# The low part of a weight block: a subtraction on DVE, or a negated copy on ACT and an adding DMA

## The chip, the cores and the metric

The kernel runs on one core of one Trainium2 chip. The core has a matrix engine (PE), a vector engine (DVE), an activation engine (ACT), a general engine (POOL), an engine that here only issues transfers (SP), and 16 DMA engines that carry the transfers of all queues. Each engine works through its own list of instructions in order; an instruction starts when the semaphores it names have reached their values. The metric is the device time of one execution in microseconds (us), as the median of several runs.

## The reference

Four layers of a transformer over 512 tokens of width 1024, all in float32: two layers with a mixer, a cross attention and a feed-forward network (FFN), then two layers with another mixer and an FFN. Cut to the part that the change is about:

```
def _conv_ffn(h, w_in, conv_w, conv_b, w_out):      # first two layers, D_FF = 2816
    gate, up = split(h @ w_in, 2)
    gate = causal_dwconv(gate, conv_w, conv_b)
    return (gelu(gate) * up) @ w_out

# each of the last two layers (mixer, then FFN of the same width)
    g = sigmoid(gate_logit)                         # three gates of width 1024 from h @ w_in
    merged = g[0] * y_attn + g[1] * y_conv + g[2] * y_pool
    x = x + merged @ w_o
    gt, up = split(rmsnorm(x) @ w_ffn_in, 2)
    x = x + (silu(gt) * up) @ w_ffn_out
```

## The kernel before

**Products in three parts.** Every operand of a large product is cut in two float32r tiles: the high part `hi` (a rounding copy on ACT, L167) and the low part `lo = src - hi` (a subtraction on DVE, L168). A product is then three matmuls, high by high, high by low, low by high (`mm3`, L248). `split` (L166) makes the two parts of any operand.

**Seven products.** The four FFNs and the gates of the two later mixers multiply a 2x2 arrangement of weight blocks with a 2x2 arrangement of activations by a scheme that needs seven block products in place of eight, at the cost of sums of blocks. `plan_seven` (L464) loads four weight blocks of 128x1024 float32 (512 KB each), called g1, g2, u1, u2, makes four sums in place on DVE (`add`, L470: first s1 = u1 + u2, then u1 = g1 - u1 and g1 = s1 - g1, later g2 = g2 - g1) and has seven blocks cut by `cut` (L450): U1 = g1, U2 = g2, U3 = the new g1, U4 = s1, U5 = the new u1, U6 = u2, U7 = the new g2. `seven` (L498) multiplies them one after the other on PE, two column halves of 12 matmuls each, and between them ACT copies partial sums out of PSUM (L512, L521, L528) and DVE adds others to them (L517, L529, L536). In the fifth product the copy L528 takes the sum out of a PSUM tile into which the sixth product then accumulates, so that the sixth product cannot start on a half before that half's L528 is done.

**FFN.** Each pair of hidden blocks is one `seven`, and after each follows `second` (L575), the product of an earlier group's hidden blocks with one or two loaded blocks of `w_out`, called w8 and w9 here. These two are loaded and cut by `unit` (L206), not by `cut`. An FFN has one plain start (four cuts) and ten `seven`; behind the first two of them `second` takes one block, behind the other eight two.

**Buffers.** The raw blocks lie in two rings: "raw" with three buffers (g2, u2, w8, w9 and their like take turns) and "rb" with four (g1, u1, s1). A load is issued on SP (L447 in `block`, L211 in `unit`) once the last reader of its buffer is done. SP's list is in order, so a load that waits holds back those behind it. The cut parts lie in five buffers each ("whi", "wlo"), a sixth one is added in the gates. A cut may start when PE has done with the block five before it.

**Order.** `Feed` keeps four cut units ahead of PE; the scheduler of the language then sets each engine's order once, when the program is built.

Of the kernel before, what the change touches and what calls it, by code (L numbers as in the profile page):

```python
# [9 lines left out]
F32 = mybir.dt.float32  # L10
# [4 lines left out]
AF = mybir.ActivationFunctionType  # L15
ALU = mybir.AluOpType
# [85 lines left out]
class Core:  # L102
# [347 lines left out]
    def cut(self, t):  # L450
        self.turn = (self.turn + 1) % 6
        pool, bufs = (self.extra, 1) if self.extra and self.turn == 0 else (self.wp, 5)
        hi = pool.tile([P, 1024], F32R, tag="whi", name=self.nm("wh"), bufs=bufs)
        lo = pool.tile([P, 1024], F32R, tag="wlo", name=self.nm("wl"), bufs=bufs)
        self.split(hi, lo, t)
        return hi.rearrange("p (k c) -> p k c", k=4), lo.rearrange("p (k c) -> p k c", k=4)

    def prod(self, out, u, c, bh, bl, start=True, stop=True, more=False):
# [1240 lines left out]
```

## Time and profile before

| what | value |
|---|---|
| median of 3 runs | 3035.33 us (3033.89 to 3038.63) |
| profiled execution | 3036.64 us |
| its span, first to last instruction | 3034.9 us |
| PE busy | 2985.4 us, 98% of the span |
| DVE busy | 2265.0 us, 75% |
| ACT busy | 1512.8 us, 50% |
| POOL busy | 66.5 us, 2% |
| DMA traffic | 317.45 MB, 105 GB/s on average |

The span is one execution seen by the profiler; what is missing to the profiled execution's own time (1.7 us) lies before the first and after the last instruction. Busy shares are averages over very different stages. A row of a list by engine gives start, duration, engine, line, operation, output and inputs; in square brackets stands how long the engine was idle before it and whose end released it. The chain of waits is the list of steps, followed back from the last instruction, each of which had to end before the next could start.

### The profile page before, as it was taken

The page shows a single profiled execution, that of the slowest core. Times are in us where ns is not written, and L with a number is a line of the kernel's source. Part 1 is how long each engine was busy: PE and PEld are TensorE (multiplying, and loading weights), DVE is VectorE, ACT ScalarE, POOL GpSimd, SP SyncE. Part 2 cuts the span into 40 slices and gives each one's busy share as a digit, 9 for nine tenths or more (in the row PEclk, how much of TensorE's full clock was granted, in tenths as well). Part 3 has the DMA queues.
Part 4 walks back from the last instruction along what each step waited for, and adds up shares of the span by engine and source line. Part 5 has one row for each costly group of instructions (what it writes and reads, how often), then busy time and mean ns, then how long its engine had stood idle before and what let it go on. Part 6 is the DMA issues. An engine that isn't in the chain of part 4 may idle for free.

```text
span 3034.9 us, 46642 instructions
## 1 busy us (share of the span) xinstructions
PE 2985.4 (98%) x18376; PEld 2613.1 (86%) x18376; DVE 2265.0 (75%) x4188; ACT 1512.8 (50%) x2475; POOL 66.5 (2%) x99
## 2 busy tenths in 40 slices
PE   8999999999999999999999999999999999999999
PEld 6888888999887788899988699899998779889998
DVE  6855768888776676888878588687777768777775
ACT  6634545545544554554454465454445555554442
POOL 1300000000000000000000000000001000000000
PEclk9999999999999999999999999999999999999999
DMA  5122522333332352233334143323334223423332
GB/s 181 36 85 97 178 87 88 103 103 105 100 123 70 105 189 97 74 114 98 105 126 119 31 125 105 129 91 105 103 105 127 87 63 122 132 91 98 104 105 77
DMA packets 232896, 317.45 MB, mean 105 GB/s; under 512 B 10805, under 2 KB 165927, under 8 KB 231781
## 3 DMA queue, kind: packets, MB, share of 16 engines
q1 hardware_dynamic: 224933, 292.20, 30.8%
q0 software_dynamic: 7744, 22.27, 2.3%
q8 instruction: 144, 2.36, 0.3%
q14 instruction: 75, 0.61, 0.1%
HBM read 294.49 MB, written 15.75 MB: 102 GB/s over the span
## 4 chain that ended last, share of the span: by engine, by line
PE 85%; DVE 9%; DMA 3%; ACT 2%; issue 1%; POOL 0%; SPq 0%; DVEq 0%; ACTq 0%
PE mm L248 58%; PE at L248 19%; PE at L203 3%; DVE wl L168 2%; PE at L1210 2%; DVE wr L470 1%; DMA wr<-in_w_ffn_in 1%; DMA wr<-in_ffn_w_in 1%; DMA wr<-in_w_in 1%; ACT wh L167 1%; PE at L696 0%; PE at L853 0%; DMA wr<-in_w_o 0%; DVE big L168 0%; DVE x L546 0%
## 5 line engine op out<-in xcount | busy, mean ns | idle before, releaser
L168 DVE TENSOR_TENSOR wl<-wr,wh 128x1024 fp32r<-128x1024 f32 (+1 forms) x678 | 817.7, 1213 | 311.0 <-ACT wh L167 301.3
L167 ACT CAST wh<-wr 128x1024 fp32r<-128x1024 f32 (+1 forms) x678 | 700.5, 1042 | 523.4 <-PE mm L248 307.4
L248 PE MATMUL mm<-Hh,wh 128*128 128x256 f32 (+1 forms) x2256 | 677.5, 300 | 3.7 <-DVE u L529 2.4
L248 PE MATMUL mm<-Hh,wl 128*128 128x256 f32 (+1 forms) x2256 | 674.5, 299 | 0.0
L248 PE MATMUL mm<-Hl,wh 128*128 128x256 f32 (+1 forms) x2256 | 674.1, 299 | 0.0
L248 PEld LDWEIGHTS mm<-Hh,wh 128*128 128x128 f32 x2256 | 423.8, 188 | 25.5 <-DVE u L529 4.1
L248 PEld LDWEIGHTS mm<-Hl,wh 128*128 128x128 f32 x2256 | 423.8, 188 | 23.6 <-issue 4.9
L248 PEld LDWEIGHTS mm<-Hh,wl 128*128 128x128 f32 x2256 | 425.5, 189 | 19.7 <-issue 2.4
L248 PE MATMUL mm<-wh,Hh 128*128 128x512 f32 x896 | 358.6, 400 | 1.5 <-ACT Hh L167 1.5
L248 PE MATMUL mm<-wh,Hl 128*128 128x512 f32 x896 | 353.8, 396 | 0.8 <-DVE Hl L168 0.8
L248 PE MATMUL mm<-wl,Hh 128*128 128x512 f32 x896 | 353.2, 394 | 0.0
L248 PE MATMUL mm<-big,wh 128*128 128x256 f32 x1920 | 341.8, 280 | 6.3 <-ACT u L528 5.0
L248 PEld LDWEIGHTS mm<-big,wh 128*128 128x128 f32 x1920 | 290.5, 188 | 11.9 <-ACT u L528 6.2
L470 DVE TENSOR_TENSOR wr<-wr,wr 128x1024 f32<-128x1024 f32 x208 | 253.8, 1220 | 53.2 <-DMA wr<-in_w_ffn_in 28.4
L248 PE MATMUL at<-wl,ah 128*128 128x512 f32 x704 | 276.8, 393 | 0.0
L248 PE MATMUL at<-wh,al 128*128 128x512 f32 x704 | 276.0, 392 | 0.0
L248 PE MATMUL at<-wh,ah 128*128 128x512 f32 x704 | 275.2, 391 | 0.0
L248 PE MATMUL mm<-big,wl 128*128 128x256 f32 x960 | 266.6, 278 | 0.4 <-DVE wl L168 0.2
L248 PEld LDWEIGHTS mm<-wh,Hl 128*128 128x128 f32 x896 | 169.0, 189 | 39.7 <-DVE Hl L168 3.1
L248 PEld LDWEIGHTS mm<-wh,Hh 128*128 128x128 f32 x896 | 169.3, 189 | 36.4 <-ACT Hh L167 2.5
L248 PEld LDWEIGHTS mm<-wl,Hh 128*128 128x128 f32 x896 | 169.4, 189 | 35.0
L248 PEld LDWEIGHTS mm<-big,wl 128*128 128x128 f32 x960 | 181.2, 189 | 0.8 <-DVE wl L168 0.8
(407 smaller groups left out, 4317.6 us busy)
## 6 DMA issues: line engine op xcount, KB each, us to landing
wr<-in_ffn_w_in SPq DMA_DIRECT2D x88, 512.0 KB
wr<-in_w_ffn_in SPq DMA_DIRECT2D x88, 512.0 KB
wr<-in_w_in SPq DMA_DIRECT2D x84, 512.0 KB
wr<-in_ffn_w_out SPq DMA_DIRECT2D x44, 512.0 KB
wr<-in_w_ffn_out SPq DMA_DIRECT2D x44, 512.0 KB
wr<-in_ev_w_in SPq DMA_DIRECT2D x32, 512.0 KB
wr<-in_xa_w_kv SPq DMA_DIRECT2D x32, 512.0 KB
wr<-in_od_w_in SPq DMA_DIRECT2D x24, 512.0 KB
```

What stands on the lines that cost most here:

```text
L167: self.nc.scalar.copy(out=hi, in_=src)
L168: self.nc.vector.tensor_tensor(out=lo, in0=src, in1=hi.bitcast(F32), op=ALU.subtract)
L203: return self.nc.tensor.transpose(out=out, in_=in_, identity=self.ident)
L248: return self.nc.tensor.matmul(*args, **kw, skip_group_check=more)
L470: self.nc.vector.tensor_tensor(out=out, in0=a, in1=b, op=op)
L1210: nc.tensor.matmul(out[:, i * P:], lhsT=v[:, i, h * width:(h + 1) * width], rhs=pT[:, OFF[i]:OFF[i] + S - i * P], start=i == 0, stop=i == ...
```

## The change

`cut` no longer calls `split`. ACT makes the high part as before, then writes the negated high part to the low tile (`activation` with `AF.Copy` and scale -1), and then POOL issues a DMA that adds the raw block to that tile in place. `unit`, `split` for activations and all loads stay as they are.

```diff
     def cut(self, t):
         ...
         hi = pool.tile([P, 1024], F32R, tag="whi", name=self.nm("wh"), bufs=bufs)
         lo = pool.tile([P, 1024], F32R, tag="wlo", name=self.nm("wl"), bufs=bufs)
-        self.split(hi, lo, t)
+        nc = self.nc
+        nc.scalar.copy(out=hi, in_=t)
+        nc.scalar.activation(out=lo, in_=hi.bitcast(F32), func=AF.Copy, scale=-1.0)
+        nc.gpsimd.dma_start(out=lo, in_=t, accum_op=ALU.add)
         return hi.rearrange("p (k c) -> p k c", k=4), lo.rearrange("p (k c) -> p k c", k=4)
```

The lines behind the change move down by three (L167 of `cut` becomes L456 and L457, L512 becomes L515, L521 becomes L524, L528 becomes L531). The program now has 380 DMAs of the new kind.

Place 1: ACT in the FFN of the second layer (the other FFNs repeat it), from the cut of U6 to the second L528 of one `seven`. Before (wh2098 is U6's high part, wh2100 U7's, wh2103 and wh2106 those of w8 and w9, wh2112 the next step's U1; wr is the raw block, DMAHW a wait on a load):

```order
L167 CAST wh2098_12975<-wr2072_12788 128x1024 [waits DMAHW6_49,PE_49]
L512 COPY g2092_12927<-mm2091_12926 128x256 [waits PE_49]
L167 CAST wh2100_13005<-wr2070_12784 128x1024 [waits DVE_49,PE_49]
L521 COPY g2089_12911<-mm2088_12910 128x256 [waits PE_49]
L167 CAST wh2103_13034<-wr2102_13033 128x1024 [waits DMAHW7_49,PE_49]
L521 COPY g2092_12927<-mm2091_12926 128x256 [waits PE_49]
L167 CAST wh2106_13068<-wr2105_13067 128x1024 [waits DVE_49,DMAHW2_49,PE_49,Activation_49]
L528 COPY u2090_12912<-mm2088_12910 128x256 [waits PE_49]
L167 CAST wh2112_13105<-wr2108_13097 128x1024 [waits DMAHW0_49,DVE_49,PE_49]
L528 COPY u2093_12928<-mm2091_12926 128x256 [waits PE_49]
```

Now, the same stretch:

```order
L456 CAST wh2098_13079<-wr2072_12887 128x1024 [waits DMAHW6_49,PE_49]
L515 COPY g2092_13030<-mm2091_13029 128x256 [waits PE_49]
L457 ACTIVATE wl2099_13080<-wh2098_13079 128x1024 [waits DMASW0_49,Activation_49]
L456 CAST wh2100_13110<-wr2070_12883 128x1024 [waits DVE_49,PE_49]
L457 ACTIVATE wl2101_13111<-wh2100_13110 128x1024 [waits DMASW1_49,PE_49,Activation_49]
L524 COPY g2089_13014<-mm2088_13013 128x256 [waits PE_49]
L167 CAST wh2103_13140<-wr2102_13139 128x1024 [waits DMAHW7_49,PE_49]
L524 COPY g2092_13030<-mm2091_13029 128x256 [waits PE_49]
L167 CAST wh2106_13174<-wr2105_13173 128x1024 [waits DMAHW2_49,PE_49]
L531 COPY u2090_13015<-mm2088_13013 128x256 [waits PE_49]
L456 CAST wh2112_13211<-wr2108_13203 128x1024 [waits DMAHW0_49,PE_49]
L531 COPY u2093_13031<-mm2091_13029 128x256 [waits PE_49]
```

Behind each cast of a cut stands a negated copy, and the cast of w9 (wh2106) still stands ahead of L531.

Place 2: SP in the same step, the loads of w8 (wr2102), the next g1 and u1 (wr2108, wr2110), w9 (wr2105) and the next g2 and u2 (wr2109, wr2111). Before:

```order
L211 DMA wr2102_13033<-in_ffn_w_out 128x2x512 [waits DMAHW4_49,DVE_49]
L447 DMA wr2108_13097<-in_ffn_w_in 128x4x256
L447 DMA wr2110_13101<-in_ffn_w_in 128x4x256 [waits DMAHW2_49,DVE_49,Activation_49]
L211 DMA wr2105_13067<-in_ffn_w_out 128x2x512 [waits DMAHW6_49,DVE_49]
L447 DMA wr2109_13099<-in_ffn_w_in 128x4x256 [waits DMAHW5_49,DMAHW3_49,DVE_49]
L447 DMA wr2111_13103<-in_ffn_w_in 128x4x256 [waits DMAHW7_49,DVE_49]
```

Now (DMASW is a wait on a DMA that POOL issued):

```order
L211 DMA wr2102_13139<-in_ffn_w_out 128x2x512 [waits DMAHW4_49,DVE_49]
L447 DMA wr2108_13203<-in_ffn_w_in 128x4x256 [waits DMASW5_49]
L447 DMA wr2110_13207<-in_ffn_w_in 128x4x256 [waits DMASW2_49,DMAHW2_49,DVE_49,Activation_49]
L211 DMA wr2105_13173<-in_ffn_w_out 128x2x512 [waits DMAHW6_49,DMASW5_49,Activation_49]
L447 DMA wr2109_13205<-in_ffn_w_in 128x4x256 [waits DMAHW7_49,DMAHW3_49,DVE_49]
L447 DMA wr2111_13209<-in_ffn_w_in 128x4x256 [waits DMAHW5_49,DMASW6_49]
```

The order of the loads is the same; w9's load (wr2105) and u2's (wr2111) wait for an adding DMA where they waited for DVE.

## Rows read from the trace of the kernel before

**Rows 1.** Page, busy us, share of the span, instructions.

```profile
PE 2985.4 (98%) x18376; PEld 2613.1 (86%) x18376; DVE 2265.0 (75%) x4188; ACT 1512.8 (50%) x2475; POOL 66.5 (2%) x99
```

**Rows 2.** Page, the chain that ended last, by line.

```profile
PE mm L248 58%; PE at L248 19%; PE at L203 3%; DVE wl L168 2%; PE at L1210 2%; DVE wr L470 1%; DMA wr<-in_w_ffn_in 1%; DMA wr<-in_ffn_w_in 1%; DMA wr<-in_w_in 1%; ACT wh L167 1%; PE at L696 0%; PE at L853 0%; DMA wr<-in_w_o 0%; DVE big L168 0%; DVE x L546 0%
```

**Rows 3.** Groups of instructions: count, busy us, mean ns, idle before, releasers.

```profile
L168 DVE TENSOR_TENSOR wl<-wr,wh 128x1024 fp32r<-128x1024 f32 (+1 forms) x678 | 817.7, 1213 | 311.0 <-ACT wh L167 301.3
L167 ACT CAST wh<-wr 128x1024 fp32r<-128x1024 f32 (+1 forms) x678 | 700.5, 1042 | 523.4 <-PE mm L248 307.4
L470 DVE TENSOR_TENSOR wr<-wr,wr 128x1024 f32<-128x1024 f32 x208 | 253.8, 1220 | 53.2 <-DMA wr<-in_w_ffn_in 28.4
```

**Rows 4.** Windows: us, busy of PE, PEld, DVE, ACT, POOL; clock, DMA share, GB/s.

```profile
655.60:686.20 30.60, 30.60 (x219) 28.46 (x218) 25.06 (x34) 15.06 (x22) 0.00 (x0) 1.00 0.32 104
655.60:675.00 19.40, 19.40 (x169) 19.25 (x168) 14.00 (x17) 9.50 (x14) 0.00 (x0) 1.00 0.47 154
1743.00:1895.00 152.00, 148.00 (x1119) 139.29 (x1118) 129.74 (x168) 86.96 (x137) 0.00 (x0) 1.00 0.37 111
```

**Rows 5.** ACT in order of time, one step of the first FFN.

```profile
654.84 2.03 ACT L167 CAST wh<-wr 128x1024 fp32r<-128x1024 f32 x2
657.20 0.37 ACT L512 COPY g<-mm 128x256 f32<-128x256 f32 x1 [0.33 <-PE mm L248]
658.45 1.05 ACT L167 CAST wh<-wr 128x1024 fp32r<-128x1024 f32 x1 [0.87 <-PE mm L248]
659.40 0.36 ACT L512 COPY g<-mm 128x256 f32<-128x256 f32 x1
661.17 1.05 ACT L167 CAST wh<-wr 128x1024 fp32r<-128x1024 f32 x1 [1.40 <-PE mm L248]
666.61 1.05 ACT L167 CAST wh<-wr 128x1024 fp32r<-128x1024 f32 x1 [1.40 <-PE mm L248]
668.08 0.37 ACT L528 COPY u<-mm 128x256 f32<-128x256 f32 x1 [0.42 <-PE mm L248]
```

**Rows 6.** DVE in the same step.

```profile
659.53 1.23 DVE L168 TENSOR_TENSOR wl<-wr,wh 128x1024 fp32r<-128x1024 f32 x1 [0.76 <-ACT wh L167]
```

**Rows 7.** SP's DMA issues in the same step.

```profile
660.79 0.37 SPq L211 DMA_DIRECT2D wr<-in_ffn_w_out  x1
```

**Rows 8.** PE in the same step, the start of the sixth product.

```profile
669.24 0.39 PE L248 MATMUL mm<-big,wh 128*128 128x256 f32 x2
```

**Rows 9.** Chain of waits in order of time, an earlier step of that FFN.

```profile
572.03 1.15 DVE wl L168
573.17 0.02 SPq L211
...
573.23 3.65 DMA wr<-in_ffn_w_out
...
577.85 1.03 ACT wh L167
578.88 0.28 ACT u L528
579.16 0.04 issue
579.21 4.37 PE mm L248 x36
```

**Rows 10.** Waits of the SP queue: us in total, times, longest.

```profile
SPq L211 <- DVE wl L168: 801.1, 151, 38.3
SPq L447 <- DVE wl L168: 562.2, 109, 32.3
```

**Rows 11.** DMA issues: count, KB each, median us to landing.

```profile
xd<-x POOLq DMA_DIRECT2D x5, 2048.0 KB, 8.6
mt<-memT POOLq DMA_DIRECT2D x2, 1024.0 KB, 6.0
td<-big POOLq DMA_DIRECT2D x4, 512.0 KB, 3.1
self<-in_c_sel POOLq DMA_DIRECT2D x2, 512.0 KB, 3.8
poolc<-in_c_pool POOLq DMA_DIRECT2D x2, 17.0 KB, 2.2
```

**Rows 12.** DMA queues: packets, MB, share of 16 engines' span.

```profile
q0 software_dynamic: 7744, 22.27, 2.3%
```

**Rows 13.** Waits of PE: us in total, times, longest.

```profile
PE mm L248 <- ACT u L528: 11.3, 11, 2.0
PE mm L248 <- DVE u L529: 2.4, 5, 0.9
```

## The prediction

> **What bounds the kernel now.** I read the page's busy shares first. PE is busy 2985.4 of 3034.9 us, DVE 75%, ACT 50% [rows 1]: 49.5 us are all that PE stands idle. The chain of waits by line says the same: matmuls at L248 take 77% of it, the subtraction that the change removes (DVE wl L168) 2%, the high-part copy 1% [rows 2]. The windows then show one FFN step (a `seven` of 19.4 us, then a `second` of 11.2 us): PE is busy for all of its 30.6 us, DVE for 25.06, ACT for 15.06, and the DMA engines for a third [rows 4]. In that stage DVE has slack already, so taking work from it buys nothing directly. Only in the gates does PE miss time, 4 us of 152 [rows 4].
>
> The waits of the SP queue are the view that matters most: loads waited for "DVE wl L168" 801 and 562 us in total [rows 10]. A raw buffer becomes free when the subtraction has read it, and only then is the next load issued. These waits cost nothing as long as the load still lands in time. The chain in order of time shows where it does not quite: a subtraction ends, SP issues the load of a `w_out` block, the load lands 3.65 us later, ACT casts it (1.03 us), ACT then does the copy L528, and PE starts the sixth product [rows 9]. PE waited for L528 11.3 us in all [rows 13]. This is the path on which the new operation lies.
>
> **What is removed and added.** L470 ran 208 times, four sums to a `seven` [rows 3]: 52 of them with seven cuts each, and four plain starts with four each, are 380 cuts. DVE loses 380 x 1.213 = 461 us [rows 3] and falls to 59% of the span. ACT gains 380 negated copies. None is in the trace; the cast of the same shape took 1.04 us [rows 3], four copies of 128x256 would take 4 x 0.37 = 1.48 us [rows 5], none could be free. I take 1.04, so 395 us, which puts ACT at 63%, and in the gates at (86.96 + 42 x 1.04) / 152 = 86% [rows 4]. Its busy time alone binds nothing, but its order does: in the list each negated copy stands among PSUM copies for which PE waits.
>
> The 380 adding DMAs have no counterpart in the trace. A POOL transfer of 17 KB landed 2.2 us after its issue, 512 KB in 3.1 or 3.8, 1024 KB in 6.0, 2048 KB in 8.6 [rows 11]. So about 2.2 us are fixed, and a pass over 512 KB takes 0.9 to 1.6 us; POOL's queue gives the same upper figure, 22.27 MB in 2.3% of 3034.9 us, 1.64 us for 512 KB [rows 12]. An addition has to read the raw block and also the tile that it adds to, so I count two passes: 1.8 to 3.3 us, and take 2.5, between the two rows of 512 KB doubled. The bounds are one pass (0.9) and three, with the write apart (3 x 1.64 = 4.9).
>
> The Trainium skill bears on this. "Collectives: The Full Stack", section "The bandwidth ceiling: the fold count and why AG ≠ RS ≠ AR", says that the DMA engines' inline addition is not slow by its arithmetic but by its two source reads, which halve the rate; no run here shows it yet. "DMA: Bandwidth & Descriptors", section "Anatomy of one DMA — SWDGE (gpsimd) path", gives about 2.0 us plus bytes at 436 GB/s for a POOL transfer; for 1024 KB that is an estimate of 4.4 us where the trace had 6.0 [rows 11], and 3.2 us for 512 KB beside 3.1. By that figure the pass would be 1.2 us, two of them 2.4, and the sum below would hardly move.
>
> **The FFN step, followed through.** T = 655.6 is the start of a `seven`. Casts of U4 and U5 ran at 654.84, back to back; that of U6 at 658.45, when PE had freed its slot; that of w9 at 666.61; L528 at 668.08; the sixth product began at 669.24 [rows 5, 8]. In the new ACT list a negated copy follows each cast, so: cast U4 to 655.9, its negation to 656.9, cast U5 to 658.0, the PSUM copy to 658.3, negation U5 to 659.4, cast U6 to 660.4, PSUM copy to 660.8, negation U6 to 661.85. Before, U6's subtraction was done at 659.53 + 1.23 = 660.76, and SP issued w9's load at 660.79 [rows 6, 7].
>
> Now the adding DMAs. With 2.2 us fixed and 2.5 us on the engines, one behind the other: U4 lands at 661.6, U5 at 664.1, U6 at 666.6, U7 at 669.1. PE needs the low part of U4 at about 664.1, of U5 at 666.9, U6 at 669.5, U7 at 672.3 (19.4 / 7 = 2.77 us to a product): all in time. What is late is the load behind U6: w9's load goes out at 666.65 instead of 660.79. It lands 3.65 us later [rows 9], plus some 1.2 us since U7's addition has half of the engines then; cast 1.03 and L528 0.28 follow. Sum: 666.65 + 3.65 + 1.2 + 1.03 + 0.36 = 672.9, against 669.24: PE stands still for 3.6 us. Behind the waiting cast of w9 on ACT stand both L528 and the next step's U1; behind w9's load on SP stand the next g2 and u2. The stall recurs, since the chain starts anew at each step when PE frees U6's slot. Break-even is an addition landed 2.3 us after its issue.
>
> Of the 40 FFN steps 32 have a w9: 32 x 3.6 = 115 us. The other eight have no second `w_out` block; I take nothing for them (at most the same, 29 us). DVE's in-place sums must now wait until an addition has read the block; U1's negation ends some 3 us after its cast in the pause before `second`, and I take nothing for it either.
>
> **The gates.** There `seven` follows `seven` with little between. U7's addition lands at T + 13.5; the next load into that buffer lands at T + 18.4; its cast, negation (2.1) and addition (4.7) end at T + 25.2, and the second product of the next `seven` wants it at T + 19.4 + 2.8 = T + 22.2. That is 3 us for each of the 12, 36 us. The engines' own load gives a floor: 0.37 x 152 = 56 us of loads [rows 4] plus 42 x 2.5 = 105 us are 161 us in a stage of 152, 9 us each; the larger figure stands.
>
> **The sum.** 3036.6 us (the profiled execution, 1.3 above the median) + 115 + 36 = 3188; less 1.3 and rounded, 3190 us, 5% slower. With 1.8 us on the engines the same steps give a stall of 2.5 us and 0.8 us in a gate `seven`: 82 + 10, 3128 us. With 3.3 us U6 lands at 669.0, the stall is 6.5 us and a gate `seven` loses 7.4: 207 + 89, 3333 us. So 3125 to 3335 is this case's own range.
>
> **Rivals.** *The DMA engines become the bound.* With 4.9 us for an addition an FFN step needs 0.32 x 30.6 + 7 x 4.9 = 44 us of engines in 30.6 us [rows 4], 13.5 us too many in each of 40 steps, and each gate stage 56 + 206 - 152 = 110 us: 540 + 220, about 3800 us. For it: 380 additions are more than POOL's queue ever carried [rows 12]. Against it: nothing here shows three passes. It decides from about 2.9 us an addition, in the gates from 2.3.
>
> *The addition is cheap and hidden.* At one pass (0.9 us) U6 lands at 664.95, the stall is some 1.2 us: 3075 us. With 2 us more slack than I count (a load that lands sooner, another order on SP) nothing is left and the time stays at 3035. For it speaks that td landed in 3.1 us [rows 11]; against it, that the second operand must be read.
>
> *Faster, by the relief of DVE.* The chain of rows 9 begins with DVE's subtractions. If an addition landed in under 2.3 us, loads would go out earlier than now, the 11.3 and 2.4 us of PE's waits for L528 and L529 [rows 13] would go, and the gates' 2 x 4 us: 3015 us. PE's idle 49.5 us are the limit of any gain.
>
> That the change does not do what it says is excluded by the order of the program.
>
> **Chances and range.** Forecast (3125 to 3335) 0.51; DMA-bound (above 3335) 0.25; cheap and hidden 0.18, of which 0.06 ends within 0.2% of now, about what a measurement of this kernel tells from no change; faster 0.06. So faster 0.06, same 0.06, slower 0.88. The range runs from 3050 to 3650 us: below it lie the faster case and no change, above it the far end of the DMA-bound case.
>
> **What would show it.** In the new profile: PE idle of 100 to 200 us with "ACT u L531" as its foremost releaser; SP's L211 waiting on the adding DMAs; a landing of the new POOL issues between 4 and 7 us; POOL's queue above 20% of the engines; DVE near 60%. Wrong would be the forecast if PE's idle time stood in front of the low parts themselves (a matmul that waits for wl), or if the DMA share were above 90% in the FFN windows.

## The result, and the profile after

The changed kernel takes 3474.29 us (3471.37 to 3478.24, 4 runs) against 3035.69 for the kernel before: 1.1445 times as long, with a 95% interval of 1.1425 to 1.1464. The forecast was 3190 us. The direction held and the time lies inside the range, but the loss is 439 us where 155 were forecast.

On the page of the changed kernel the first line is busy time by engine, then come the queue that carries POOL's transfers and the issues of the adding DMAs with their median landing:

```profile
PE 3120.0 (90%) x18376; PEld 2731.5 (79%) x18376; DVE 1846.7 (53%) x3808; ACT 1860.9 (54%) x2855; POOL 397.7 (11%) x479
...
q0 software_dynamic: 62464, 221.53, 33.0%
...
wl<-wr POOLq DMA_DIRECT2D x380, 512.0 KB, 5.9
```

Beside [rows 1], DVE lost 418 us of work and ACT gained 348. PE does the same 18376 matmuls, yet its busy time rose from 2985.4 to 3120.0 us, and its idle time from 49.5 to 349.6 us (3469.6 of span less 3120.0). These two, 134.6 and 300.1 us, are the whole 434.7 us by which the span grew. PE's waits in the changed kernel (us in total, times, longest) answer to [rows 13]:

```profile
PE mm L248 <- ACT u L531: 191.4, 40, 6.8
PE mm L248 <- DMA wl<-wr: 78.2, 52, 4.7
PE mm L248 <- ACT b L167: 17.7, 4, 5.5
PE mm L248 <- DVE ac L549: 9.9, 5, 3.4
```

The copy named in the forecast leads. Next come waits for the adding DMAs themselves, of which there were none before. The group of matmuls that the FFNs' seven products alone have shows how much of the first row is theirs (count, busy us, mean ns, idle before):

```profile
L248 PE MATMUL mm<-big,wh 128*128 128x256 f32 x1920 | 410.4, 316 | 170.8 <-ACT u L531 165.8
```

So 165.8 of the 191.4 us belong to the FFNs, and 25.6 to the gates. The waits for wl are 22.5 us in the FFNs' seven products, 42.0 us in the gates, and 13.7 us at the FFNs' starts.

The chain of waits in order of time shows one such stall in the third FFN, piece by piece, as [rows 9] does for before:

```profile
2359.95 6.99 DMA wl<-wr
2366.94 0.02 SPq L211
...
2366.99 3.85 DMA wr<-in_w_ffn_out
...
2370.92 0.07 ACT wh L167
...
2371.87 0.37 ACT u L531
...
2372.29 8.36 PE mm L248 x48
```

It reads as forecast: U6's addition lands 6.99 us after its issue, SP issues w9's load, that lands 3.85 us later, ACT casts w9, then copies, then PE starts. PE's own rows put its idle time before that start at 4.14 us:

```profile
2372.29 0.80 PE L248 MATMUL mm<-big,wh 128*128 128x256 f32 x2 [4.14 <-ACT u L531]
```

What PE does then is in the windows (us, busy of PE, PEld, DVE, ACT, POOL with counts, clock, DMA share, GB/s), the first just before the stall, the second just behind it:

```profile
2360.00:2367.90 7.90, 7.90 (x72) 7.90 (x71) 1.65 (x2) 3.61 (x5) 1.69 (x2) 1.00 1.02 191
2372.30:2377.60 5.30, 5.30 (x25) 5.30 (x26) 4.04 (x5) 2.12 (x3) 0.87 (x1) 0.50 0.73 231
```

After 4.14 us at rest the granted clock is at its lower level, 0.50 (1.2 GHz), for 5.3 us: 25 matmuls took 5.3 us, where 72 took 7.9 before. At the earlier pace the 25 would have taken 2.7 us, so the stall costs 2.6 us again as PE busy time. The first copy L531 of two successive steps, in ACT's rows of the first FFN, gives the length of a step:

```profile
679.46 0.37 ACT L531 COPY u<-mm 128x256 f32<-128x256 f32 x1
...
717.04 0.37 ACT L531 COPY u<-mm 128x256 f32<-128x256 f32 x1
```

That is 37.6 us, against 30.6 [rows 4]. The new instructions by group (count, busy us, mean ns, idle before):

```profile
L458 POOL DMA_DIRECT2D wl<-wr x380 | 331.0, 872 | 2208.7 <-ACT wl L457 1446.8
...
L457 ACT ACTIVATE wl<-wh 128x1024 fp32r<-128x1024 f32 x380 | 400.2, 1060 | 6.8 <-issue 2.4
```

The engine time of one addition follows from the queue: 33.0% of 3469.6 us is 1145 us; less the 70 us that the same queue had before [rows 12], divided by 380, it is 2.83 us.

The trace also has the landing of each addition and the time of each DMA packet. In the 40 FFN steps the addition of U3, which finds the queue free, lands 4.55 us after its issue in the median; those of U4 to U7, issued close together, take 4.89, 5.70, 6.23 and 7.09. For the 32 loads of w9, the median time from the issue to the end of the load's last packet is 3.32 us before and 4.70 now.

### The profile page after: what moved, and what is told of

Same layout as the page of the kernel before. It is cut to its first block, busy times and chain, and to the rows that moved or that the text cites. A ratio compares the mean times of both kernels' runs of the same rounds, so it can differ in the third digit from the quotient of the medians.

```text
span 3469.6 us, 48042 instructions
## 1 busy us (share of the span) xinstructions
PE 3120.0 (90%) x18376; PEld 2731.5 (79%) x18376; DVE 1846.7 (53%) x3808; ACT 1860.9 (54%) x2855; POOL 397.7 (11%) x479
## 5 line engine op out<-in xcount | busy, mean ns | idle before, releaser
L168 DVE TENSOR_TENSOR wl<-wr,wh 128x1024 fp32r<-128x1024 f32 (+2 forms) x298 | 358.2, 1204 | 568.7 <-ACT wh L167 558.7
L458 POOL DMA_DIRECT2D wl<-wr x380 | 331.0, 872 | 2208.7 <-ACT wl L457 1446.8
L248 PE MATMUL mm<-big,wh 128*128 128x256 f32 x1920 | 410.4, 316 | 170.8 <-ACT u L531 165.8
L456 ACT CAST wh<-wr 128x1024 fp32r<-128x1024 f32 x380 | 394.2, 1046 | 314.7 <-PE mm L248 102.1
L167 ACT CAST wh<-wr 128x1024 fp32r<-128x1024 f32 (+2 forms) x298 | 305.8, 1032 | 402.2 <-DMA wr<-in_ffn_w_out 120.9
L248 PEld LDWEIGHTS mm<-big,wh 128*128 128x128 f32 x1920 | 349.8, 225 | 178.2 <-ACT u L531 172.5
L248 PEld LDWEIGHTS mm<-Hh,wh 128*128 128x128 f32 x2256 | 435.1, 193 | 49.4 <-DVE g L539 11.3
L457 ACT ACTIVATE wl<-wh 128x1024 fp32r<-128x1024 f32 x380 | 400.2, 1060 | 6.8 <-issue 2.4
L248 PE MATMUL mm<-big,wl 128*128 128x256 f32 x960 | 299.8, 312 | 10.6 <-DMA wl<-wr 10.4
L248 PEld LDWEIGHTS mm<-big,wl 128*128 128x128 f32 x960 | 215.4, 224 | 13.2 <-DMA wl<-wr 13.2
```

The lines of the kernel that those rows point to most:

```text
L167: self.nc.scalar.copy(out=hi, in_=src)
L168: self.nc.vector.tensor_tensor(out=lo, in0=src, in1=hi.bitcast(F32), op=ALU.subtract)
L248: return self.nc.tensor.matmul(*args, **kw, skip_group_check=more)
L456: nc.scalar.copy(out=hi, in_=t)
L457: nc.scalar.activation(out=lo, in_=hi.bitcast(F32), func=AF.Copy, scale=-1.0)
L458: nc.gpsimd.dma_start(out=lo, in_=t, accum_op=ALU.add)
```

## The experiments

Each loss is taken from the median of the kernel before in the same comparison (3028 to 3041 us). U1 to U7, w8 and w9 are named as above.

**1. The same engines without the DMA.** ACT negates, DVE adds. The ACT list keeps its order around w9's cast and the copies.

```diff
-        nc.gpsimd.dma_start(out=lo, in_=t, accum_op=ALU.add)
+        nc.vector.tensor_tensor(out=lo, in0=t, in1=lo.bitcast(F32), op=ALU.add)
```

> The negated copy stays on ACT, the addition is made by DVE (lo = raw + lo) and not by a DMA. Theory of the held buffer (the loss comes from the raw block that the adding DMA holds until it lands, so that the next load, ACT's cast and the copy L531 come late): the buffer of U6 is free about 2.3 us later than before, within the slack of 3.4 us that the load of w9 has, so 3035 to 3070 us, no PE waits above 1 us at L531 in the FFN steps, granted clock 1.00. Rival, ACT's list (380 more copies of 1.06 us in front of the PSUM copies are the cost): at least 3200 us.

3052.06 us, ratio 1.0046 (1.0031 to 1.0061). Its page has

```profile
PE 2989.4 (98%) x18376; PEld 2611.1 (86%) x18376; DVE 2274.0 (75%) x4188; ACT 1857.7 (61%) x2855; POOL 66.6 (2%) x99
```

so 345 us more on ACT cost 16 us. The rest of the loss, 423 of 439 us, comes with the DMA.

**2. Which stages.** `cut` uses the DMA in the gates' seven products alone, else `split`.

```diff
-        self.split(hi, lo, t)
+        if dma:                      # true in the gates only
+            nc.scalar.copy(out=hi, in_=t)
+            nc.scalar.activation(out=lo, in_=hi.bitcast(F32), func=AF.Copy, scale=-1.0)
+            nc.gpsimd.dma_start(out=lo, in_=t, accum_op=ALU.add)
+        else:
+            self.split(hi, lo, t)
```

> The adding DMA in the gates' twelve seven-products alone (84 additions), the FFNs as before. Splits the loss by stage: read from the changed kernel's starts the gates lost 52 to 57 us each, so 3140 us; the prediction's own term was 36 us, 3072 us. If the gates lose time only because the FFNs before them end late, 3040 us.

3144.21 us, 1.0372 (1.0353 to 1.0391): 112 us for the gates. By difference some 326 are left for the FFNs and the four plain starts; no run has the FFNs alone. PE's waits in this run:

```profile
PE mm L249 <- DMA wl<-wr: 40.0, 23, 4.5
PE mm L249 <- ACT u L535: 27.3, 12, 6.1
```

In the gates PE waits first for the low parts. Its busy time is 3022.3 us on this run's page, 37 more than before.

**3. A buffer of its own for w9,** so that its load waits for no addition.

```diff
-        raw = self.wp.tile([P, 1024], F32, tag="raw", name=self.nm("wr"), bufs=3)
+        raw = (pool.tile([P, 1024], F32, tag="rw", name=self.nm("wr"), bufs=1) if pool else
+               self.wp.tile([P, 1024], F32, tag="raw", name=self.nm("wr"), bufs=3))   # pool given for w9 only
```

> The second w_out block of an FFN step (w9) gets a raw buffer of its own, so that its load waits no longer for the addition of U6; all else as in the changed kernel. Theory of the held buffer: PE's wait for L531 (191 us in 40 waits) goes almost wholly, with it the low clock behind it, and 200 to 250 us come back: 3220 to 3290 us. Rival, the DMA engines bound the FFN (their share is 0.77 to 0.87 there): PE waits as long for other things, at least 3400 us, DMA share above 0.9.

3416.42 us, 1.1235 (1.1212 to 1.1258). Only 58 us came back, and the DMA share in the FFN windows was 0.81 to 0.86, not above 0.9. Its chain of waits shows why (w9's cast is on time, at 2346.84):

```profile
2346.84 1.06 ACT wh L167
...
2348.86 5.01 DMA wr<-in_w_ffn_in
...
2353.97 1.24 DVE wr L474
...
2356.45 0.35 DVE u L533
...
2356.84 2.67 PE mm L249 x12
```

Now the next step's blocks are late, and their in-place sums (L474) stand ahead of the add L533 in DVE's list. The wait moved from ACT to DVE: PE waited 106.3 us for L533, and 58.6 for the ACT copy. The chain does not name what kept the late block from being issued sooner; the waits of the SP queue do (us in total, times, longest). In this run:

```profile
SPq L448 <- DMA wl<-wr: 1399.8, 106, 26.9
```

In the changed kernel:

```profile
SPq L447 <- DMA wl<-wr: 1079.2, 107, 25.9
```

So this run does not take the hold away. It frees one buffer, and the next loads wait longer for the additions that still hold the others.

**4. A late w9 without additions.** The kernel before with w9 loaded three times into its buffer.

```diff
-        self.nc.sync.dma_start(out=raw[:, :n].rearrange(...), in_=src.rearrange(...))
+        for _ in range(1 + more):    # more = 2 for w9
+            self.nc.sync.dma_start(out=raw[:, :n].rearrange(...), in_=src.rearrange(...))
```

> The kernel before, with subtraction on DVE, but each w9 is loaded three times in a row into the same buffer, so that it lands about 7.3 us later. No adding DMA in it. Theory: w9 lands at 671.75 in the step that starts at 655.6, PE stands still for 3.9 us a step at L528, 32 steps, 125 us; the granted clock falls after each such stall and adds some 2.7 us a step, 86 us: 3230 to 3260 us. Rival, the clock falls by the adding DMAs or ACT's work and not by PE's stall: 3150 to 3170 us at a granted clock of 1.00. Rival, late loads do not matter: 3035 us.

3071.13 us, 1.0109 (1.0094 to 1.0125). A miss, and no test of the theory: the order on ACT changed with the edit.

```profile
2086.17 0.37 ACT L529 COPY u<-mm 128x256 f32<-128x256 f32 x1 [2.88 <-PE mm L249]
2087.53 0.37 ACT L529 COPY u<-mm 128x256 f32<-128x256 f32 x1 [0.99 <-PE mm L249]
2092.80 2.95 ACT L167 CAST wh<-wr 128x1024 fp32r<-128x1024 f32 x3 [4.90 <-DMA wr<-in_w_ffn_out]
```

The cast that waits for w9 now stands behind both copies, and the late load costs 35 us. With the cast in that place a late w9 does little harm; what it does with the cast ahead of the copy is not tested here.

**5. U6's addition alone,** the other cuts by DVE.

```diff
+        if dma and 6 in WHICH: ...   # WHICH = (6,), FFN only: 40 additions
```

> Only the sixth cut (u2) of the FFN's seven products is made with the negated copy and the adding DMA, 40 additions in all; the other cuts have the subtraction on DVE. Held-buffer theory: w9's load still waits for that addition (some 5 us to landing, on free engines), so PE waits about 3 us for the copy behind w9's cast in 32 steps, and loses as much again by the lower granted clock behind it: 3130 to 3220 us. Rival, the DMA engines' load: 40 additions are 113 us of engines in all, no stage is short of them, 3035 to 3060 us.

3087.00 us, 1.0182 (1.0164 to 1.0201). U6's addition alone, with its hold, its own load on the engines and 40 negated copies, costs 55 us: less than the held-buffer theory's 95 to 185, more than the rival's 0 to 25. Neither range has it.

**6. The load without the hold.** The kernel before, plus 380 additions of a cut's high part to scratch tiles in DRAM.

```diff
         self.split(hi, lo, t)
+        j = self.junk[self.jn % 8]
+        self.nc.gpsimd.dma_start(out=j, in_=hi.bitcast(F32), **({"accum_op": ALU.add} if self.jn >= 8 else {}))
+        self.jn += 1
```

> The kernel before, its subtraction on DVE kept, plus 380 adding DMAs of the same 512 KB: each adds the high part of a cut to a scratch tile in DRAM that nobody reads, so no raw block is held by it. Held-buffer theory (the time is lost because a raw block stays taken until its addition has landed): 3040 to 3110 us, PE idle under 90 us. Rival, the DMA engines' load alone (loads land late because additions use the engines): 3250 us or more, with the DMA share of the FFN near 0.85 as in the changed kernel.

3372.82 us, 1.1141 (1.1110 to 1.1172): 341 of the 439 us, with nothing held and DVE as before. The held buffer cannot be the whole cause. The scratch tiles lie in DRAM, where the changed kernel adds within SBUF: the engine time of an addition is the same (34.4% of 3363.4 us, less 70, by 380, is 2.86 us), but it lands 7.7 us after its issue in the median, not 5.9. No run adds to scratch tiles in SBUF. The chain shows the same stall with another cause:

```profile
2298.60 1.06 ACT wh L168
...
2299.69 1.23 DVE wl L169
2300.91 0.03 DVE g L521
2300.94 11.26 DMA wr<-in_w_ffn_out
...
2313.25 0.37 ACT u L532
...
2313.67 6.43 PE mm L249 x42
```

w9's load goes out at once behind U6's subtraction, as before the change, but takes 11.26 us in place of 3.65 [rows 9]. In the changed kernel the addition and then the load took 6.99 + 3.85 = 10.84 us: nearly the same delay, once in the queue of the buffer and once in that of the engines. Over all 32 loads of w9, issue to end of the last packet, the median is 8.92 us here, against 3.32 before and 4.70 in the changed kernel. POOL's rows of that step:

```profile
2295.94 0.86 POOL L458 DMA_DIRECT2D junk<-wh  x1 [8.82 <-ACT wh L168]
2297.31 0.86 POOL L458 DMA_DIRECT2D junk<-wh  x1 [0.51 <-ACT wh L168]
2299.95 0.86 POOL L458 DMA_DIRECT2D junk<-wh  x1 [1.78 <-ACT g L516]
2302.67 0.86 POOL L458 DMA_DIRECT2D junk<-wh  x1 [1.86 <-ACT wh L168]
```

Four additions, some 11 us of engine time, go out within 6.7 us around w9's load: three in the 5 us ahead of it, one behind it. In this step the first of the load's 256 packets began 2.44 us after the issue and the last ended at 10.59, so the packets themselves were late, not only the word that they had landed. Between 2 and 6 us after the issue 125 packets of the load and 132 of the additions began, almost one for one.

**7. The source in DRAM.** The additions of U1, U2 and U6 read the weights once more.

```diff
-        nc.gpsimd.dma_start(out=lo, in_=t, accum_op=ALU.add)
+        nc.gpsimd.dma_start(out=lo.rearrange(...), in_=src.rearrange(...), accum_op=ALU.add)   # for g1, g2, u2
```

> The changed kernel, but the adding DMAs of U1, U2 and U6 take the weight block from DRAM once more and not from the raw buffer, which ACT's cast alone then holds. Same work of the DMA engines, less holding, w9's buffer (u2) free some 6 us sooner. Held-buffer theory: 3250 us or less. DMA-load theory: like the run with an own buffer for w9 and the run with load alone, 3360 to 3430 us.

3362.80 us, 1.1063 (1.1046 to 1.1079): inside the range of the load's theory. 115 us came back (439 less 324), and 324 stay. But the test is not clean: the additions of U3, U4, U5 and U7 still hold their blocks (the next blocks' loads waited 1091.7 us for additions, 1079.2 in the changed kernel), and the additions from DRAM landed later, 8.4 and 9.4 us after their issue in the median, and PE waited 106.9 us for the low parts that are added from SBUF (78.2 in the changed kernel).

**8. One pass in place of two.** The changed kernel with a plain copy (the low tile gets the raw block), and the load alone with a plain copy.

```diff
-        nc.gpsimd.dma_start(out=lo, in_=t, accum_op=ALU.add)
+        nc.gpsimd.dma_start(out=lo, in_=t)
```

> The DMA copies the raw block over the low tile and adds nothing, so the low parts are wrong values; all waits and buffers stay. Theory of the held buffer with two passes to an addition: one pass is about 1.4 us shorter, the landing falls from 5.9 to some 3.5 to 4.5 us, PE's wait at L531 from 4.2 to 1 to 2 us a step, 3100 to 3250 us. Rival, the latency of a POOL transfer or ACT's list is the cost and not the bytes: 3400 us or more, landing above 5 us.

> As the run with load alone (subtraction on DVE, 380 transfers of a cut's high part to scratch tiles in DRAM, no raw block held), but plain copies of one pass, so that an FFN step asks 9.8 + 7 x 1.4 = 19.7 us of the DMA engines in 30.6 us. Theory now, the engines' load: the loss belongs to engines that are nearly full, so at 64% it is small, 3035 to 3100 us; the run with the plain copy that also holds the raw block (3160 us) then shows some 60 to 120 us as the price of holding. Rival, any transfer in POOL's queue delays the loads whatever its passes: 3200 us or more.

3160.52 us, 1.0412 (1.0385 to 1.0439), and 3070.00 us, 1.0103 (1.0086 to 1.0120). The queue of the first gives the engine time of a plain copy, as above: 20.3% of 3173.7 us, less 70, by 380, is 1.51 us.

```profile
q0 software_dynamic: 62464, 221.53, 20.3%
```

As many transfers of half the engine time cost 31 us by their load, and 124 with the hold. The difference is some 93 us here, and 98 between the changed kernel and run 6 (439 less 341). It is not the hold alone: the runs with it also have the negated copies (16 us in run 1), and their transfers end in SBUF where those of the other two end in DRAM.

**9. Mean load, packets, or the burst.** Scratch additions for five cuts in seven; then all of them in 1 KB packets (the scratch rows lie apart); then only U4 to U7, and only U1 to U3.

```diff
+        if self.cuts % 7 < 5: ...                              # first
+        self.nc.gpsimd.dma_start(out=j[:, :, :256], ...)       # second: j is 4 x 272 wide
+        if i in WHICH: ...                                     # (4, 5, 6, 7), and (1, 2, 3)
```

> Load alone again, with additions of two passes for five cuts in seven: 9.8 + 5 x 2.83 = 24 us of engines in a step of 30.6 us, 78%. If engines are short only where the sum passes the step: 3040 to 3080 us. If single loads land late well before that, because an addition in front of them takes the engines: 3120 to 3260 us.

3235.76 us, 1.0651 (1.0625 to 1.0678), a loss of 197 us, although the engines' time asked for leaves a fifth of the step free.

> The run with load alone and two passes (3373 us), with the rows of the scratch tile kept apart so that an addition is made of 1 KB packets, like the loads of the seven products, and no longer of 4 KB ones. If the loads are late because a small packet waits its turn behind a large adding one: the loads land sooner, 3100 to 3250 us, at an engine time per addition near 2.8 us. If only the engines' time counts: 3340 to 3420 us, or more by as much as small packets cost engine time.

3364.05 us, 1.1101 (1.1082 to 1.1119), no other than run 6, although this queue took 40.6% of 3368.8 us, 3.42 us an addition. The edit changed two things, smaller packets and a fifth more engine time, and the sum came out the same. The loads of w9 did end somewhat sooner, 7.25 us after their issue in the median where run 6 had 8.92, but PE's waits went over from the copy L532 (150.5 to 79.7 us) to the add L533 (62.7 to 137.4). So smaller packets do not win the time back; whether the two changes offset each other, no run separates.

> Load alone (nothing held, subtraction on DVE), scratch additions for U4, U5, U6 and U7 of each seven products only: 9.8 + 4 x 2.83 = 21.1 us of engines in a step of 30.6 us, 69%. Burst theory: w9's load still lands behind four additions, some 10 us after its issue, so most of the loss of the full load stays: 3200 to 3340 us. Mean-load theory, between the runs at 64% (+31 us) and 78% (+197 us): 3080 to 3160 us.

> The same with scratch additions for U1, U2 and U3 only: 9.8 + 3 x 2.83 = 18.3 us, 60%. Burst theory: no addition lies ahead of w9's load, 3035 to 3065 us. Mean-load theory: 3050 to 3080 us. A loss above 100 us would say that another load than w9's is the one that counts.

3268.80 us, 1.0754 (1.0731 to 1.0776), and 3048.93 us, 1.0027 (1.0015 to 1.0040). Four additions in seven lose 228 us, more than five spread over all cuts (197); the other three lose 8. The chain with U4 to U7:

```profile
2216.32 1.23 DVE wl L170
2217.55 0.03 DVE g L523
2217.57 10.61 DMA wr<-in_w_ffn_out
...
2229.23 0.38 ACT u L534
...
2229.65 7.34 PE mm L250 x48
```

w9's load takes 10.61 us, about as with all seven (medians of the 32 loads, issue to end of the last packet: 8.55 us here, 8.92 with all seven, 3.30 with U1 to U3). With U1 to U3 a window in the FFN reads

```profile
600.00:700.00 100.00, 100.00 (x723) 93.56 (x722) 82.00 (x108) 49.77 (x71) 7.77 (x9) 1.00 0.60 153
```

PE is full at a DMA share of 0.60. Where the additions fall counts for more than how many there are: the harmful ones are those issued close together around w9's load, in 27 of the 32 cases three in the 6 us ahead of it and one in the 3 us behind it.

**10. Work for PE during the stall.** 36 matmuls into an unused PSUM tile ahead of the sixth product of each FFN step.

```diff
+            for k in range(36):
+                nc.tensor.matmul(spare[:, :256], lhsT=u[0][:, k % 4, 0:P], rhs=B[0][0][0][:, k % 4, :], start=True, stop=True)
         u = feed.get()
```

> The changed kernel with 36 more matmuls of 128x256 into an unused PSUM tile in each FFN step, ahead of the sixth product, where PE otherwise stands still for about 4 us; their results are not used. If the low granted clock behind each stall (2.7 us of slower matmuls) is lost time of its own: PE's busy time without the added matmuls falls, and the time to 3380 to 3440 us. If the DMA engines set the step: what the clock gives back is waited for elsewhere, 3450 to 3510 us.

> The filled kernel once more, for a profile at its usual time: near 3452 us. If the clock was a loss of its own, the granted clock is up and PE's busy time without the 1440 added matmuls is well under 3120 us, while PE's idle time has grown by less than that; if the DMA engines set the step, the idle time before the low parts (wl) and the later copies has grown by as much as the clock gave back.

The first gave 3449.80 us in the median of three executions, 1.1346 (1.1318 to 1.1373); a fourth took 7957 us for a reason that stays open, and the profile is of that one, so it is not used. The second gave 3443.11 us, 1.1370 (1.1347 to 1.1392), and on its page stands

```profile
PE 3226.2 (94%) x19816; PEld 2841.0 (82%) x19816; DVE 1847.0 (54%) x3808; ACT 1860.6 (54%) x2855; POOL 398.3 (12%) x479
```

and among its groups the added matmuls:

```profile
L536 PE MATMUL at<-Hh,wh 128*128 128x256 f32 x1440 | 170.8, 277 | 0.0
```

Without the added matmuls PE is busy 3055.4 us, 65 less than the 3120.0 of the changed kernel. Of these 65 us some 24 came out as time (a loss of 415 us where the changed kernel has 439). The rest was waited for elsewhere: PE's idle time (218.1 us) and the added matmuls make 388.9 us, 39 more than the 349.6 us of idle time without them. Neither expectation holds whole.

**11. The cheap part kept.** U1 to U3 of the FFNs by the new way, all else as before.

```diff
+        if dma and i in WHICH: ...   # WHICH = (1, 2, 3), FFN only
```

> In the FFNs the first three cuts of each seven products (U1, U2, U3) by negation and adding DMA, 120 additions; U4 to U7 and the gates by DVE as before. Held-buffer theory: u2 and s1, whose late release delays w9 and the next loads, are free as early as before; what is held is g2 (U2) and g1 (U1, U3), which no early load waits for: 3020 to 3075 us. DMA-load theory: three additions of 2.8 us beside 9.8 us of loads are 18 us of a 30.6 us step, also no loss. Loss above 3100 us would speak for a third cause, the in-place sums on DVE that must wait for an addition.

3067.07 us, 1.0119 (1.0103 to 1.0136): DVE is down to 2138.9 us, and the kernel is 35 us slower. On its page PE is idle 16 us longer and busy 13 us longer; what it waits for was not followed further. No version here beats the kernel before.

## Why the prediction was right in direction and wrong in size

- *What bounds.* Right: PE was full, DVE's relief bought nothing. The rival "faster by the relief of DVE" is out: DVE fell to 53%, and run 11 loses too.
- *Negated copies, 1.04 us.* Measured 1.060; run 1 puts the price of the whole new ACT list at 16 us.
- *Two passes, 2.5 us of engines.* Measured 2.83, against 1.51 for the plain copy of run 8, so 1.9 times as much. The Trainium skill, "Collectives: The Full Stack", section "The bandwidth ceiling: the fold count and why AG ≠ RS ≠ AR", says that the inline addition costs by its second source read. This case's times agree, 2.83 to 1.51; the reads themselves stand in no trace.
- *The stall in the step.* The mechanism is the one in the chain, and it was forecast: w9's load goes out when U6's addition has landed, and took 4.70 us in the median to its last packet (in the step shown the landing came 0.4 us behind that), where 3.65 + 1.2 = 4.85 was forecast to its landing. What was mis-sized is the landing of U6's addition, 4.75 us after its issue in the forecast (661.85 to 666.6) and 6.23 in the median. For 32 steps the forecast was 115 us; PE waited 165.8 us for L531 in the FFNs, 5.2 us for each of the 32. The step shown above, with 4.14, is one of the milder ones.
- *Break-even at 2.3 us.* By the forecast's own terms, with the 1.2 us for the slower load, it is 1.1 us; 2.3 leaves that term out.
- *Low parts "all in time".* Wrong in the FFNs, by 22.5 us. In the gates the waits for wl, 42.0 us, are close to the 36 forecast.
- *The gates.* 36 us forecast, 112 measured (run 2). The forecast had the wait for wl alone. In run 2 PE's waits for wl and for the copy (67 us) and 37 us of slower matmuls make most of it. The rival's floor would have been the larger figure with the measured 2.83 us: 56 + 42 x 2.83 = 175 us of engines in a stage of 152, 23 us in each, 46 in all, still under half.
- *The step that failed* is the sum, 3036.6 + 115 + 36: it counts a stall as the time that PE stands idle, and has no term for what PE does behind it. Against its 151 us the span grew by 434.7. Of the 284 us that were missing, 134.6 are the same matmuls run slower: the granted clock was 0.50 behind the stall shown, and 0.951 in the mean of the span, against 1.000 before. The sum had put this at nothing, without a reason. Another 51 are the stall in the FFNs, by U6's late landing; 22.5 are low parts in the FFNs and 25.6 the copy L531 in the gates, both put at nothing. The rest is spread over smaller waits. The 134.6 us are not 135 us to be had: in run 10, giving back 65 of them gained 24.
- *The held buffer as the cause.* It is true of the changed kernel's chain, but not the whole cause. What goes with it is some 93 us beside plain copies and some 98 beside additions (runs 8 and 6), the negated copies included. With nothing held 341 us stay (run 6), since w9's load, issued at once, then lands nearly as late among the additions' packets. Runs 3 and 7 (380 and 324 us left) free some buffers only, and cannot tell the hold from the load.
- *The engines in the forecast.* I let the additions follow one another and land in time, since 7 x 2.5 us and 9.8 us of loads fit in 30.6. Runs 6 and 9 show that a sum over a step is the wrong test: with nothing held, four additions around w9's load stretch it from 3.32 to 8.55 or 8.92 us in the median.
- *The rival "DMA engines become the bound"* came nearer in time, though not by its arithmetic: it asked for 2.9 us an addition and a share above 0.9, and the share in the changed kernel's FFN was about 0.8. With 69% of a step's engine time asked for in the wrong places 228 us were lost, with 60% in the right ones 8.
- *Luck.* The forecast's own range ended at 3335 us, and the time is outside it. That 3474 lies in the wide range is owed to the far end of that rival, which is not what came about.

Not settled is why a load stays so long behind additions issued around it. The Trainium skill, "DMA: Bandwidth & Descriptors", section "Queues, rings and completion order", says that an engine takes the queues in turn by packets, and that a transfer's completion is written only after every earlier write of that engine, across its queues. The alternating packets of run 6 agree with the first (125 to 132). The second cannot be the main reason there: the load's own last packet ended 10.59 us after the issue, of 11.26 to the landing. Why the first packet waited 2.44 us and the last ones to 10.5 us, no run here shows.

## What to carry to other kernels

Moving elementwise work to DMA from a vector engine that has slack was no gain here. Look at what is queued around the next critical load in the few microseconds before and behind it, not at the share of the DMA engines over a step. A transfer that reads a load's buffer can delay the next load twice, by the buffer and by the engines, and in run 6 removing the first left most of the loss. Price a stall of PE with the slower matmuls behind it, but don't count on winning them back while the data is late.

## What was not expected of the hardware

- An adding DMA of 512 KB took 2.83 us of the 16 engines and 0.87 us of POOL to issue; a plain one took 1.51 and 0.53 (run 8).
- In 1 KB packets the addition took 3.42 us of the engines (run 9), against 2.86 in 4 KB ones (run 6).
- Four additions within 6.7 us around it stretched a load of 512 KB from 3.65 us to 11.26 (run 6).
- After 4.14 us at rest the granted clock stood at 0.50 for some 5.3 us.
